# First block's output projection inside the sample scan, with the gate made chunk by chunk

## The chip, the core and the metric

The kernel runs on one core of a Trainium2 chip. A core has TensorE (PE, matrix products into PSUM), VectorE (DVE), ScalarE (ACT), GpSimd (POOL), and SyncE (SP), whose queue issues most of the DMAs here. The metric is the device time of one execution in microseconds. Where several executions were timed, the median is given.

## The reference

The reference is one layer of a diffusion backbone, for 256 prompt tokens and 1024 sample tokens of width 1024, with the same weights. The part that matters here is the mixer and the way it is added to the residual:

```python
proj = h @ w_in                                   # h = rmsnorm(x) * (1 + scale) + shift
hc, gb, gc, z, xbc, dtf, dtb = split(proj)
out_a = gb * dwconv1d(gc * hc, w_conv_short)      # 512 channels
xbc = silu(dwconv1d(xbc, w_conv_ssd, b_conv_ssd))
xs, bm, cm = split(xbc)
y_f, s_f = ssd_scan(xs, dt_f, a[0], bm, cm, init_f)
y_b, s_b = ssd_scan(reversed inputs, init_b)      # backward in position
y = y_f + reversed(y_b) + xs * d_skip
y = rmsnorm(y * silu(z), g_ssd_norm)              # "gate": over 512 channels
x = x + gate_m * (concatenate([out_a, y]) @ w_out)
h2 = rmsnorm(x, g_norm2) * (1 + scale_f) + shift_f
```

`ssd_scan` works in chunks of 128 positions: inside a chunk a decay-weighted product of C and B scores with x, from chunk to chunk a state that is decayed and added to. A feed-forward part with a depthwise convolution follows, and a final norm. Outputs are both token groups and two states.

## The kernel before

All operands lie with channels on partitions and tokens along the free axis. A projection splits each fp32 operand into a high and a low part in fp32r and makes three products (hi x hi, hi x lo, lo x hi). `mm3` issues them. `wload` loads a weight tile (`raw`, 128x1024), ACT copies its high half (`whi`), VectorE or GpSimd makes the low half (`wlo`).

The stages in order of time: norm of the inputs; the prompt's input projections; the sample's projections for x, B and C (`xbc`), with the conditioning products (`ada`) between them; the backward scan (`ssd_pass1`), which only stores chunk states; the forward scan (`ssd_pass2`), which makes the outputs; the gate; the output projection; the feed-forward part in two column groups.

`ssd_pass2` goes in half-chunk steps: a chunk of 128 tokens has two groups of four heads, and each is one step `i`, so the prompt has 4 steps and the sample 16. `front(c)` transposes a chunk's x and B, makes the scores and, with `state_step`, the next state. `prep(u, g)` loads `csb` (the cumulative log decays of eight rows, spread over all partitions by a DMA of 512 KB, two buffers), adds a mask into `wm`, takes exponentials on ACT and multiplies; `output(u, g)` makes 12 small matmuls into `yp` and VectorE adds them onto the tile `xs`. `prep` runs two steps ahead of `output`.

`fill(s, i)` is called ahead of each `output` and puts one more of the 16 remaining input projections (z and the three parts of the short convolution, made by the generator `fillers`) into the step, so that TensorE has work while the chain of `csb` runs. It does this at even `i` of the prompt and at `i % 3 != 2` of the sample. The rest of them follows the scan. The short convolution's result goes to DRAM as high and low parts (`oad`, tiles `xl`), the z projections as they are (`zd`).

After the scan `gate(s, behind)` works on whole token groups: it reads z back, applies Silu, multiplies, sums squares into one tile, takes the sum over channels by a matmul with ones, scales, and writes the high and low parts of y into SBUF tiles (`mya`, `myb`). Then `wout` makes the output projection in two column groups, A with 704 tokens and B with 576, eight output blocks each, from 16 operand tiles: eight of y, eight of the short convolution read back from `oad` (`oa`, `ob`). The residual x is loaded again (`x1`) to be added to. All these tiles come from pools that open when those of the scan close.

The order on each engine comes from a scheduler that works with priorities and with `after(mm, behind)`, which keeps a matmul behind another one. DMAs on a queue are issued in the order of its instructions, so a DMA that waits holds back those behind it.

The names that are used below: `wm`, `csb` (L562 to L573), `yp` (L592), `acc` (a projection's PSUM tile, L147 to L151), `gate` (L700 to L719), `oa`, `x1`, `ob` (L739, L742, L746).

Of the kernel before, what the change touches and what calls it, by code (L numbers as in the profile page):

```python
# [53 lines left out]
def body(nc, tc, A):  # L54
# [6 lines left out]
    def open_pool(name, side="left", **kw):  # L61
        g = tc.tile_pool(name=name, bufs=1, side=side, **kw)
        return g, g.__enter__()
# [53 lines left out]
    g_xy, xy = open_pool("xy", side="right")  # L117
# [24 lines left out]
    def mm3(outs, wh, wl, n):  # L142

        mms = []
        for k in range(n):
            for o, rh, rl in outs:
                nc.tensor.matmul(o, wh[:, k, :], rh(k), start=k == 0, stop=False)  # L147
            for o, rh, rl in outs:
                nc.tensor.matmul(o, wh[:, k, :], rl(k), start=False, stop=False)  # L149
            for o, rh, rl in outs:  # L150
                mm = nc.tensor.matmul(o, wl[:, k, :], rh(k), start=False, stop=k == n - 1)  # L151
            mms.append(mm)
        return mms
# [100 lines left out]
    def ada_block(k):  # L254
        wa = [T(xy, [P, 4, 2 * P], "xs", 4) for _ in range(2)]
        for i in range(2):
            dma(wa[i], A["w_ad1"][k, i])
        pm = psa()
        for j in range(KT):
            q = 32 * (j % 4)  # L260
            nc.tensor.matmul(pm[q:q + 32, 0:2 * P], sc[:, j, :], wa[j // 4][:, j % 4, :],
# [70 lines left out]
    oad = T(dr, [4, 2, P, TT], "oad", 1)  # L332
    zd = T(dr, [4, P, TT], "zd", 1)
# [38 lines left out]
    def zproj(s, j, lo_eng):  # L372
        pp = proj(s, 12 + j, lo_eng)
        z = T(cv, [P, s.T], "xl", 2)
        act(z, pp, AF.Copy)
        nc.scalar.dma_start(zd[j, :, s.t0:s.t0 + s.T], z)
# [105 lines left out]
    def tok_major(s, c, want_raw, r0):  # L482
# [10 lines left out]
        xd = T(sw[0], [P, 512], "xd", 4)  # L493
# [3 lines left out]
        if want_raw:  # L497
            xtok = T(sw[0], [P, 512], "xd", 4)
            act(xtok, xt, AF.Copy)
        return btok, xd, xtok  # L500

    def state_step(s, c, st, btok, xd, r0, tag):
        ad = psa()
        for g in range(2):
            nc.tensor.matmul(ad[:, g * 256:(g + 1) * 256], btok[:, g, :],
                             xd[:, g * 256:(g + 1) * 256], start=True, stop=True)
# [9 lines left out]
    def ssd_pass1(s):  # L516

        st = [None]

        def step(c):  # L520
            if st[0] is not None:
                dma(s.sbd[c], st[0])
            if c > 0 or s.name == "p":
                btok, xd, _ = tok_major(s, c, False, 32)
                st[0] = state_step(s, c, st[0], btok, xd, 32, "sb")
# [6 lines left out]
        return [lambda c=c: step(c) for c in range(s.nc - 1, -1, -1)]  # L532

    def ssd_pass2(s, fill):
# [7 lines left out]
        def front(c):  # L542
# [12 lines left out]
            if c < s.nc - 1 or s.name == "p":  # L555
                sf[0] = state_step(s, c, sf[0], btok, xd, 0, "sfw")
# [45 lines left out]
        for g in range(2):  # L602
            prep(u, g)
        for i in range(2 * s.nc):
            output(*us[i], fill(s, i))
# [19 lines left out]
    SS.X = [T(xy, [P, TS], "xs", 4) for _ in range(4)]  # L625
# [10 lines left out]
    silu = act(bcall, bcall, AF.Silu)  # L636
    for j in range(4):
# [8 lines left out]
    dts = dtstage(SS, d4_s, silu)  # L646
# [3 lines left out]
    SS.B, SS.C = bcs[0:2], bcs[2:4]  # L650
    for i in range(N_LOOP, 8):
# [3 lines left out]
        if i >= 4:  # L655
            ada(i - 2, lambda: T(nrm, [P, 1024], "x", 8))
# [3 lines left out]
    mask = sm[:, wff0:wff0 + 2 * L].rearrange("p (a l) -> p a l", a=2)  # L660
    dma(mask, A["cst"][:, 168:168 + 256].rearrange("p (a l) -> p a l", a=2))
    SP.mask = SS.mask = mask

# [9 lines left out]
    def fill(s, i):  # L673

        if i % 2 == 0 if s.name == "p" else i % 3 != 2:
            next(filler, None)
            return mid_mm[0]
        return last_mm[-1]

    for step in ssd_pass1(SS) + ssd_pass1(SP):  # L680
        step()
    ssd_pass2(SP, fill)
    ssd_pass2(SS, fill)
    for _ in filler:
# [3 lines left out]


    g_ya, ya = open_pool("ya")  # L690
    g_yb, yb = open_pool("yb")
    g_gt, gt_ = open_pool("gt")
    mya = [[T(ya, [P, TA], "ya", 8, F32R) for _ in range(2)] for _ in range(4)]
    myb = [[T(yb, [P, OB], "yb", 8, F32R) for _ in range(2)] for _ in range(4)]
    def gate(s, behind):
        n = s.T
        acc = T(gt_, [P, n], "gq", 3)
        for j in range(4):
            z = T(gt_, [P, n], "gz", 2)
            dma(z, zd[j, :, s.t0:s.t0 + n])  # L700
            act(z, z, AF.Silu)
            tt(s.X[j], s.X[j], z, ALU.mult)
            if j == 0:
                act(acc, s.X[j], AF.Square)
            else:
                q = T(gt_, [P, n], "gq", 3)
                sq = act(q, s.X[j], AF.Square)
                tt(acc, acc, q, ALU.add)
        r = T(gt_, [P, n], "gq", 3)
        rstd(r, acc, n, pst, 512, sq, behind)  # L710
        for j in range(4):
            y = s.X[j]
            stt(y, y, smv("gsd")[:, j:j + 1], r, ALU.mult, ALU.mult)
            parts = [(0, n, mya, s.t0)] if s.name == "p" else \
                [(0, TA - TP, mya, TP), (TA - TP, TS, myb, 0)]
            for a, b, dst, o in parts:
                hi = dst[j][0][:, o:o + b - a]
                act(hi, y[:, a:b], AF.Copy)  # L718
                tt(dst[j][1][:, o:o + b - a], y[:, a:b], hi.bitcast(F32), ALU.subtract)  # L719
    with tc.high_priority():  # L720
        gate(SP, last_mm[-5])
        gate(SS, last_mm[-3])
    close_pool(g_xy)

    close_pool(g_gt)
# [394 lines left out]
```

## Time and profile before

| | us |
|---|---|
| median of 3 runs | 1625.38 |
| lowest and highest | 1622.09, 1627.95 |
| the profiled execution, its own time | 1629.9 |
| its span in the profile | 1628.1 |
| granted TensorE clock, mean | 0.978 |

The profile is that of one execution of its own. The page gives busy time by engine; a window is a stretch of the span with the busy time of each engine in it; a row of waits tells which instruction waited, for which, how long in all, how often, and the longest. "PEclk" is the clock that TensorE was granted, as a share of the full one. "DMA share" is the mean busy share of the core's 16 DMA engines.

### The profile page before, as it was taken

Reading aid. Unit: us, or ns where it says so; the run is one execution under the profiler, and the core shown is the slowest. Engines: PE = TensorE matmul, PEld = TensorE weight load, DVE = VectorE, ACT = ScalarE, POOL = GpSimd, SP = SyncE. Lnnn points to the kernel's source line nnn. Section 1 sums busy time; section 2 is a strip of 40 time slices with the busy share of each in tenths; the row PEclk is TensorE's granted clock in tenths of the full one; section 3 lists DMA queues with packets and bytes.
Section 4 is the critical chain, followed back from the end, with each engine's and each line's share of the span. In section 5 each row is a group of like instructions: output and inputs, shape, how many; then the busy total and the mean of one; then the engine's idle time right before and its main releaser. Section 6 shows DMA issues by size and latency. Waiting matters only on the chain. (4 is left out here: it accounts for less than half of the span.)

```text
span 1628.1 us, 24939 instructions
## 1 busy us (share of the span) xinstructions
PE 1548.7 (95%) x9942; PEld 1411.9 (87%) x9942; DVE 1095.6 (67%) x1637; ACT 646.3 (40%) x1005; POOL 519.1 (32%) x288
## 2 busy tenths in 40 slices
PE   6989999888899799999999999999999999999997
PEld 2688767677777689999999999999999999999996
DVE  5664625445555636698666697656798777887685
ACT  6553534344445424343333353323334232433233
POOL 0445010011111000234434443434455444444442
PEclk8999999999999899999999999999999999999998
DMA  8555275534333551422222243222622223332221
GB/s 295 208 182 162 73 255 191 155 99 78 105 115 128 198 197 53 131 73 86 65 85 79 70 156 115 77 70 70 200 94 92 89 82 98 125 114 73 84 62 65
DMA packets 99534, 193.19 MB, mean 119 GB/s; under 512 B 9274, under 2 KB 51786, under 8 KB 99418
## 3 DMA queue, kind: packets, MB, share of 16 engines
q1 hardware_dynamic: 97690, 188.46, 35.9%
q10 hardware_dynamic: 1728, 3.15, 0.5%
q8 instruction: 78, 1.28, 0.3%
q14 instruction: 38, 0.31, 0.1%
HBM read 167.89 MB, written 23.67 MB: 118 GB/s over the span
## 5 line engine op out<-in xcount | busy, mean ns | idle before, releaser
L76 DVE SCALAR_TENSOR_TENSOR cc<-acc,sm,cc 128x384 f32<-128x384 f32 (+7 forms) x836 | 547.1, 665 | 114.8 <-ACT cc L855 44.9
L73 POOL TENSOR_TENSOR wlo<-raw,whi 128x1024 fp32r<-128x1024 f32 (+2 forms) x115 | 271.6, 2362 | 848.2 <-ACT whi L137 707.7
L137 ACT ACTIVATE whi<-raw 128x1024 fp32r<-128x1024 f32 x126 | 133.1, 1057 | 319.0 <-PE acc L149 279.6
L147 PE MATMUL acc<-ya,whi 128*128 128x256 f32 (+2 forms) x768 | 178.8, 315 | 10.7 <-ACT yb L718 7.7
L149 PE MATMUL acc<-ya,whi 128*128 128x256 f32 (+2 forms) x768 | 178.6, 314 | 0.0
L151 PE MATMUL acc<-ya,wlo 128*128 128x256 f32 (+2 forms) x768 | 177.7, 313 | 0.0
L149 PE MATMUL acc<-oa,whi 128*128 128x256 f32 (+2 forms) x768 | 176.3, 311 | 0.0
L151 PE MATMUL acc<-oa,wlo 128*128 128x256 f32 (+2 forms) x768 | 175.9, 311 | 0.0
L147 PE MATMUL acc<-oa,whi 128*128 128x256 f32 (+2 forms) x768 | 175.8, 311 | 0.0
L76 DVE SCALAR_TENSOR_TENSOR x<-dn,mod,x 128x320 f32<-128x320 f32 (+2 forms) x176 | 96.1, 546 | 91.8 <-PE dn L151 91.1
L147 PEld LDWEIGHTS acc<-ya,whi 128*128 128x128 f32 x768 | 138.8, 191 | 14.0 <-ACT yb L718 8.1
L149 PEld LDWEIGHTS acc<-ya,whi 128*128 128x128 f32 x768 | 139.5, 191 | 3.5 <-issue 0.2
L151 PEld LDWEIGHTS acc<-ya,wlo 128*128 128x128 f32 x768 | 139.1, 191 | 3.4 <-issue 0.2
L151 PEld LDWEIGHTS acc<-oa,wlo 128*128 128x128 f32 x768 | 137.6, 189 | 3.0
L147 PEld LDWEIGHTS acc<-oa,whi 128*128 128x128 f32 x768 | 137.5, 189 | 3.0
L149 PEld LDWEIGHTS acc<-oa,whi 128*128 128x128 f32 x768 | 137.5, 189 | 3.0
L73 POOL TENSOR_TENSOR dlo<-draw,dhi 128x512 fp32r<-128x512 f32 (+1 forms) x88 | 107.7, 1225 | 78.1 <-ACT dhi L912 78.1
L147 PE MATMUL acc<-h,whi 128*128 128x512 f32 x352 | 113.7, 404 | 3.8 <-DVE xs L76 3.8
L149 PE MATMUL acc<-h,whi 128*128 128x512 f32 x352 | 112.7, 399 | 0.0
L151 PE MATMUL acc<-h,wlo 128*128 128x512 f32 x352 | 112.4, 398 | 0.0
L147 PE MATMUL dn<-yb,dhi 128*128 128x320 f32 (+2 forms) x352 | 108.9, 309 | 1.8 <-DVE x L76 1.8
L151 PE MATMUL dn<-yb,dlo 128*128 128x320 f32 (+2 forms) x352 | 108.7, 309 | 0.0
(283 smaller groups left out, 3030.2 us busy)
## 6 DMA issues: line engine op xcount, KB each, us to landing
raw<-in_w_up SPq DMA_DIRECT2D x88, 512.0 KB, 3.5
x<-in_w_ada SPq DMA_DIRECT2D x32, 512.0 KB, 7.4
draw<-in_w_down SPq DMA_DIRECT2D x64, 256.0 KB, 2.8
x<-in_w_in SPq DMA_DIRECT2D x24, 512.0 KB, 4.0
raw<-in_w_in SPq DMA_DIRECT2D x22, 512.0 KB, 4.5
xs<-in_w_ad SPq DMA_DIRECT2D x16, 512.0 KB, 5.1
csb<-csds SPq DMA_DIRECT2D x16, 512.0 KB, 9.1
raw<-in_w_out SPq DMA_DIRECT2D x16, 512.0 KB, 3.6
```

What stands on the lines that cost most here:

```text
L73: (eng or V).tensor_tensor(out=out, in0=a, in1=b, op=op)
L76: V.scalar_tensor_tensor(out=out, in0=a, scalar=s, in1=b, op0=op0, op1=op1)
L137: act(hi, raw, AF.Copy)
L147: nc.tensor.matmul(o, wh[:, k, :], rh(k), start=k == 0, stop=False)
L149: nc.tensor.matmul(o, wh[:, k, :], rl(k), start=False, stop=False)
L151: mm = nc.tensor.matmul(o, wl[:, k, :], rh(k), start=False, stop=k == n - 1)
```

## The change

The gate of the sample is made per chunk inside the scan, its result goes to DRAM (`yd`, as high and low parts) and is read back as operand tiles. All 16 remaining projections stand in the backward scan and in the first half of the sample's forward scan. Group A of the output projection is cut into 32 quarter blocks of 12 matmuls, and three of them stand in each of the last eight sample steps. In detail:

- Pools get `reuse_waits="tile"`: a new tile waits for the old tiles in its place, not for all of a closed pool. `xy` moves to the left side, `xs` tiles come in pairs, the mask has a tile of its own, `xd` has 3 buffers and not 4, and the feed-forward part uses one pool `ma` of 16 tiles in the places of `ya` and `oa`.
- z gets its Silu right after its projection on ACT, and its store goes to SP's queue. The sample's dt stage stands behind the last of these Silu. The ada blocks stand at i = 2, 3, 5, 6 (before: 4 to 7).
- The backward scan runs the prompt first, in pairs of chunks with one projection between a pair's transposes and its state products. In the forward scan the state product comes behind the step's projection or output-projection step.
- `wlo` of group A is made on GpSimd; the order of the operand tiles is 4, 5, 6, 0, 1, 2, 3, 7.

```diff
     def open_pool(name, side="left", **kw):
+        if "space" not in kw:
+            kw["reuse_waits"] = "tile"
...
-        act(z, pp, AF.Copy)
-        nc.scalar.dma_start(zd[j, :, s.t0:s.t0 + s.T], z)
+        s.zact = act(z, pp, AF.Silu)
+        dma(zd[j, :, s.t0:s.t0 + s.T], z)
...
+        u.step(last_mm[-1])
         for i in range(2 * s.nc):
-            output(*us[i], fill(s, i))
+            behind = fill(i)
+            if i % 2 == 1 and i + 1 < 2 * s.nc:
+                u.step(behind)
+            output(*us[i], behind)
...
-    dts = dtstage(SS, d4_s, silu)
+    dts = dtstage(SS, d4_s, SP.zact)
...
+    ADA = {2: 2, 3: 3, 5: 4, 6: 5}
     for i in range(N_LOOP, 8):
...
-        if i >= 4:
-            ada(i - 2, lambda: T(nrm, [P, 1024], "x", 8))
+        if i in ADA:
+            ada_s(ADA[i])
...
+    def gate_chunk(c, hr):
+        cl = slice(c * L, (c + 1) * L)
+        tl = slice(TP + c * L, TP + (c + 1) * L)
+        zu = T(xy, [P, 8, L], "xp", 1, F32R)
+        z, u = zu[:, 0:4].bitcast(F32), zu[:, 4:8]
+        uf = u.bitcast(F32)
+        dma(z, zd[:, :, tl].rearrange("j p t -> p j t"))
+        for q in range(2):
+            tt(uf[:, 2 * q:2 * q + 2], xpair[q][:, :, cl], z[:, 2 * q:2 * q + 2], ALU.mult)
+        act(z, uf, AF.Square)
+        tt(z[:, 0:2], z[:, 0:2], z[:, 2:4], ALU.add)
+        pp = psa()
+        for i in range(2):
+            mm = nc.tensor.matmul(pp[:, 0:L], ones, z[:, i], start=i == 0, stop=i == 1)
+            if i == 0:
+                after(mm, last_mm[-1])
+        hi, r = hr[:, 0:4], hr[:, 4].bitcast(F32)
+        act(r, pp[:, 0:L], AF.Ln, scale=1.0 / 512, bias=epsc)
+        act(r, r, AF.Exp, scale=-0.5)
+        for j in range(4):
+            stt(uf[:, j], uf[:, j], smv("gsd")[:, j:j + 1], r, ALU.mult, ALU.mult)
+        act(hi, uf, AF.Copy)
+        tt(u, uf, hi.bitcast(F32), ALU.subtract)
+        for i, src in enumerate((hi, u)):
+            dma(yd[:, i, :, tl].rearrange("j p t -> p j t"), src.bitcast(F32))
+    KS_A = [4, 5, 6, 0, 1, 2, 3, 7]
+    def open_mix():
+        close_pool(g_cv)
+        close_pool(g_hs)
...
+        ph.mix = {k: mix_load(ph.ma, "ya", 16, TA, k, 0, TA) for k in KS_A}
+        ph.x1 = [T(ph.x1p, [P, TT], "x1", 8) for _ in range(KT)]
+        for k in range(KT):
+            dma(ph.x1[k], xT[:, k, :])
+    def wout_steps(mix, parts, t0, ks, alloc, eng, cuts):
+        x1 = ph.x1
+        for m in range(KT):
+            wh, wl = split_wout(m, eng)
+            pp = alloc()
+            for c in range(0, KT, cuts):
+                for k in ks[c:c + cuts]:
+                    st, sp = k == ks[0], k == ks[-1]
+                    for w, i, first, last in ((wh, 0, st, False), (wh, 1, False, False), (wl, 0, False, sp)):
+                        for p0, a, b, v in parts:
+                            mm = nc.tensor.matmul(pp[:, p0:p0 + b - a], w[:, k, :], mix[k][i][:, a:b],
+                                                  start=first, stop=last)
...
+                yield
+    N_PROJ = 8
+    N_FILL = 3
+    def fill_s(i):
+        if i == 0:
+            gate_p()
+        elif i % 2 == 0:
+            hr = T(cv, [P, 8, L], "cv", 4, F32R) if i <= N_PROJ else T(ph.gt, [P, 5, L], "hr", 1, F32R)
+            gate_chunk(i // 2 - 1, hr)
+        if i < N_PROJ:
+            project()
+            behind = mid_mm[0]
+        else:
+            if i == N_PROJ:
+                open_mix()
+                ph.steps = wout_steps(ph.mix, PARTS_A, 0, KS_A, pacc, PG, 2)
+            for _ in range(N_FILL):
+                next(ph.steps, None)
+            behind = last_mm[-1]
+        return behind
+    for i in range(0, len(scans), 2):
+        cps = [(step, c, copies(c)) for copies, step, c in scans[i:i + 2]]
+        project()
+        for (step, c, cp), behind in zip(cps, (mid_mm[0], last_mm[-1])):
+            step(c, cp, behind)
+    ssd_pass2(SP, lambda i: project() if i < 3 else last_mm[-1])
+    ssd_pass2(SS, fill_s)
+    gate_chunk(7, T(ph.gt, [P, 5, L], "hr", 1, F32R))
+    for _ in ph.steps:
+        pass
```

`mix_load` loads the high and low part of one operand tile, from `oad` for k from 4 on and from `yd` below; `gate_p` is the same gate on the prompt's 256 tokens.

How this moves instructions shows at three places. The first is SP's queue where the operand tiles and the residual are loaded. Before, they stand behind the gate, after the scan (`xl` is the last part of the short convolution, its store goes to `oad`):

```order
L746 DMA ob_4286<-oad_579 128x576
L398 DMA oad_579<-xl_4095 128x1024
L399 DMA oad_579<-xl_4097 128x1024
L739 DMA oa_4249<-oad_579 128x704
L739 DMA oa_4250<-oad_579 128x704
```

In the changed kernel the last rows of this load and the first rows behind it are, on the same queue, in the middle of the sample's scan (`ya` an operand tile, `x` the residual, `csb` the log decays of steps 10 and 11):

```order
L770 DMA ya_3952<-yd_572 128x704
L770 DMA ya_3954<-oad_571 128x704
L770 DMA ya_3956<-oad_571 128x704
L783 DMA x_624_3958<-in_xT 128x1280
L783 DMA x_625_3959<-in_xT 128x1280
L783 DMA x_626_3960<-in_xT 128x1280
L783 DMA x_627_3961<-in_xT 128x1280
L783 DMA x_628_3962<-in_xT 128x1280
L783 DMA x_629_3963<-in_xT 128x1280
L783 DMA x_630_3964<-in_xT 128x1280
L783 DMA x_631_3965<-in_xT 128x1280
L576 DMA csb_4051<-csds_569 128x8x128
```

So 16 operand tiles and eight residual tiles now stand ahead of the `csb` loads of the last six steps; before, no `csb` load stood behind either. The second place is TensorE ahead of the output of step 10. After the change the end of the output projection's fourth block (`acc_4363`) stands right ahead of that step's first matmuls:

```order
L796 MATMUL acc_4363<-ya_3956,whi_4359 128x256
L796 MATMUL acc_4363<-ya_3956,whi_4359 128x448
L796 MATMUL acc_4363<-ya_3954,wlo_4361 128x256
L796 MATMUL acc_4363<-ya_3954,wlo_4361 128x448
L606 MATMUL yp_4213<-wm_4053,xd_4046 64x128
L606 MATMUL yp_4213<-csb_4051,sfw_3862 64x128
```

Before, the first matmuls of group A stand behind the last input projection (`acc_4045`), which follows the scan and the gate's sums:

```order
L147 MATMUL acc_4045<-h_547,whi_4041 128x512 x2
L149 MATMUL acc_4045<-h_550,whi_4041 128x512 x2
L151 MATMUL acc_4045<-h_547,wlo_4043 128x512 x2
L147 MATMUL acc_4303<-ya_4112,whi_4299 128x256
L147 MATMUL acc_4303<-ya_4112,whi_4299 128x448
```

So half of group A now stands between the outputs of steps 9 and 10, and the other half around those of 10 to 15. The third place is TensorE from group A to group B (`ob`, `yb` operand tiles of B, `nacc` the squares of the second norm on A, `dn` their sum). Before, inside B's first block `acc_4863`:

```order
L151 MATMUL acc_4863<-yb_4126,wlo_4861 128x256
L151 MATMUL acc_4863<-yb_4126,wlo_4861 128x320
L147 MATMUL acc_4863<-ob_4281,whi_4859 128x256
L202 MATMUL dn_4778<-nacc_4753,ones_70 128x512
L202 MATMUL dn_4781<-nacc_4753,ones_70 128x192
L147 MATMUL acc_4863<-ob_4281,whi_4859 128x320
```

After (`sa_4664` is the sum of the last chunk's gate, from its squares `xp`):

```order
L796 MATMUL acc_4740<-ya_3954,wlo_4738 128x448
L744 MATMUL sa_4664<-xp_4658,ones_70 128x128 x2
L205 MATMUL dn_4865<-nacc_4840,ones_70 128x512
L205 MATMUL dn_4868<-nacc_4840,ones_70 128x192
L796 MATMUL acc_4950<-ob_4808,whi_4946 128x256
```

The norm's sum stood behind the first 25 matmuls of B; now both sums stand ahead of all of them. On SP's queue the loads of B's tiles stand behind the last chunk's stores to `yd`.

205 lines of the change are left out of this document (96 added, 109 removed).

## Prediction

> **What bounds the kernel now.** I read the page first, for the span and the share of TensorE.
>
> ```profile
> span 1628.1 us, 24939 instructions
> PE 1548.7 (95%) x9942; PEld 1411.9 (87%) x9942; DVE 1095.6 (67%) x1637; ACT 646.3 (40%) x1005; POOL 519.1 (32%) x288
> ...
> PEclk8999999999999899999999999999999999999998
> ```
>
> TensorE is busy for 95% of the span, nearly always at full clock. So the only time to win is where it waits or runs at half clock, and the next view has to say where that is: the busy time of each engine by stage. I cut at the start of the backward scan (258), of the sample's second scan (320), at its end (511), at the wait ahead of the output projection (547), at the projection's two column groups A (555.2) and B (624.9), and at the feed-forward part (676.8).
>
> ```profile
> core 0: us, PE busy (x) PEld busy (x) DVE busy (x) ACT busy (x) POOL busy (x), PEclk, DMA share, GB/s
> ...
> 160.00:258.00 98.00, 94.25 (x474) 65.96 (x472) 41.29 (x58) 39.23 (x43) 7.16 (x3) 0.97 0.52 183
> 258.00:320.00 62.00, 57.52 (x334) 45.56 (x332) 40.34 (x63) 28.80 (x67) 4.73 (x2) 1.00 0.49 153
> 320.00:511.00 191.00, 167.99 (x977) 135.23 (x976) 102.06 (x129) 80.64 (x175) 30.80 (x11) 0.96 0.35 95
> 511.00:547.00 36.00, 34.65 (x147) 27.17 (x146) 22.72 (x30) 24.71 (x34) 0.00 (x0) 1.00 0.44 147
> 547.00:555.20 8.20, 0.48 (x3) 0.09 (x2) 8.20 (x11) 5.29 (x10) 0.00 (x0) 0.67 0.68 216
> 555.20:624.90 69.70, 66.71 (x384) 63.15 (x385) 23.94 (x31) 13.72 (x16) 0.00 (x0) 0.92 0.54 201
> 624.90:676.80 51.90, 51.90 (x389) 51.34 (x388) 41.03 (x61) 26.48 (x36) 4.79 (x2) 1.00 0.25 80
> 676.80:1628.00 951.20, 938.42 (x6359) 917.69 (x6357) 721.62 (x1126) 342.55 (x507) 408.93 (x237) 0.99 0.30 93
> ```
>
> From 258 to 624.9 TensorE stands idle for 4.48 + 23.01 + 1.35 + 7.72 + 2.99 = 39.6 us. The granted clock adds to that: 0.96 in the scan costs 0.04 x 191 = 7.6 us, 0.92 in group A 0.08 x 69.7 = 5.6 us. Together **52.8 us** lie there, and group B has none. The feed-forward part keeps its order on every engine, so it moves as a block. TensorE's waits of 258 to 690 name the causes:
>
> ```profile
> PE yp L592 <- DVE wm L73: 9.0, 4, 5.8
> PE acc L147 <- ACT yb L718: 7.7, 1, 7.7
> PE yp L592 <- DVE xs L76: 7.2, 5, 2.2
> PE yp L592 <- DVE csb L73: 3.1, 5, 0.6
> PE acc L147 <- ACT whi L137: 3.0, 1, 3.0
> ```
>
> Columns are the waiter, the releaser, total us, times, the longest. The scan's outputs (yp) wait for the decay weights (wm, csb); the output projection waits once for the gate's last split (7.7) and once for a weight tile that lands behind the x loads (3.0).
>
> **The change, part by part.** *What goes.* Gating chunk by chunk takes the 7.7 us wait away; projections and output-projection steps in all 16 sample steps cover the yp waits. I take out the whole 52.8 us and then add what is left or new.
>
> *Ahead of the scan.* Three waits stand here now:
>
> ```profile
> PE acc L147 <- DVE xs L76: 3.8, 1, 3.8
> PE sa L475 <- DVE cv L472: 3.4, 1, 3.4
> PE acc L147 <- ACT xl L375: 3.3, 1, 3.3
> ```
>
> ```profile
> L370 ACT ACT_TABLE_LOAD x3 | 3.8, 1283 | 8.4 <-DVE xs L76 8.1 <-DVE bc L76 0.4
> ```
>
> Silu on the z projections, between the Ln and Exp of the sample's dt stage, makes six more table loads on ACT: at worst 6 x 1.283 = 7.7 us, if TensorE waits for all of them. At best the 3.4 and the 3.3 shrink, since the dt stage stands behind the last Silu and its reader later. Four ada blocks begin two steps earlier, and the weights of one stand on SP's queue behind a store that waits for VectorE. I take **+2**, with -4 and +8 as ends: ACT is busy 39.23 of 98 us in that stage, so most loads find room.
>
> *Gate sums.*
>
> ```profile
> L202 PE MATMUL yp<-gq,ones x6: 379/592/697, 520.8 to 543.0; 128*128 128x512 f32 x4, 128*128 128x256 f32 x2
> ```
>
> These sum the squares now; the new gate adds only pairs on VectorE and lets TensorE do the other half, on twice the columns. Some 4 x 0.56 us come to **+2.2**.
>
> *Backward scan and first half.* Each of the first eight sample steps now has a projection, and the state products stand behind it.
>
> ```profile
> L147 PE MATMUL acc<-h,whi 128*128 128x512 f32 x166 | 52.9, 400 | 0.0
> ```
>
> ```profile
> 369.01:379.89 10.88, 10.88 (x48) 8.93 (x48) 6.38 (x6) 2.22 (x4) 2.87 (x1) 1.00 0.49 122
> ```
>
> One projection is 48 matmuls and 10.88 us. The scan window holds 3 x 166 of them, 10.4 projections; 167.99 less the 7.6 of slow clock is 160.4, and without 10.4 x 10.88 there remain 47.2 us for 16 steps: 2.95 us of own work a step. With a projection that makes 13.8 us, in which one csb load and its exponentials fit. The idle time here is 27.5 us now, mostly in steps without a projection; I leave **+4** of it (0 to 15, if the queue also makes these steps late).
>
> *Second half.* Group A is 66.71 - 5.6 = 61.1 us, 7.64 for each of its eight output blocks and 1.91 a quarter. Eight steps of 2.95 + 3 x 1.91 and eight quarters after them are 84.7 us of work. What stands against it is SP's queue. Ahead of the csb loads of steps 10 to 15 there are 16 mix tiles and eight x tiles:
>
> ```profile
> x<-in_xT SPq DMA_DIRECT2D x8, 640.0 KB, 10.7
> oa<-oad SPq DMA_DIRECT2D x8, 352.0 KB, 4.4
> oad<-xl SPq DMA_DIRECT2D x2, 512.0 KB, 3.0
> ```
>
> ```profile
> 562.70:582.90 20.20, 20.20 (x129) 19.32 (x128) 5.44 (x9) 3.44 (x4) 0.00 (x0) 1.00 1.02 406
> ```
>
> Such loads move 406 GB/s with every DMA engine busy. 16 x 352 + 8 x 640 KB are 11.0 MB, 27 us. Seven weight tiles, two stores of the long convolution, eight of gated chunks and a few state and z tiles are about 8.1 MB, 20 us. A csb load (512 KB in pieces of 128 numbers) is another matter:
>
> ```profile
> 423.33 0.37 SPq L562 DMA_DIRECT2D csb<-csds  x1
> ...
> 427.93 0.37 SPq L562 DMA_DIRECT2D csb<-csds  x1
> ```
>
> ```profile
> 432.10 1.23 DVE L73 TENSOR_TENSOR wm<-csb,sm 128x1024 f32<-128x1024 f32 x1 [3.83 <-DMA csb<-csds]
> ...
> 435.91 0.69 DVE L73 TENSOR_TENSOR wm<-wm 128x512 f32<-128x512 f32 x1 [1.72 <-ACT wm L570]
> 438.10 1.23 DVE L73 TENSOR_TENSOR wm<-csb,sm 128x1024 f32<-128x1024 f32 x1 [1.50 <-DMA csb<-csds]
> ```
>
> ```profile
> DMA to landing us min/median/max: 5.7/8.9/10.4
> ```
>
> ```profile
> 458.00:460.00 2.00, 0.26 (x3) 0.29 (x4) 2.00 (x4) 0.88 (x1) 2.00 (x1) 1.00 0.38 82
> ```
>
> Two that were issued 4.6 us apart landed 6.0 us apart (their readers waited for them), and a lone one takes 8.9. So a csb holds the queue for 6.0 to 8.9 us. Seven of them from the eighth projection on, with 27 + 20 us of other traffic, land by 89 to 109 us. From a landing to the weights takes some 5.2 us (432.10 to 435.91 + 0.69 and one like it), then half a step, 1.5, and the 55 matmuls of A behind the last output, 8.8. A so ends at 104.5 to 124.8 against 84.7 of work: a stall of 20 to 40. I take **+24**, near the pair's 6.0, with some 4 us for loads that wait for a buffer.
>
> The Trainium skill ("DMA: Bandwidth & Descriptors", Specifications) puts the smallest transfer for line rate at 512 bytes, which is just what a csb piece has. By it a csb would go at 406 GB/s, 512 KB in 1.3 us, seven in 9, and the time would be near that of the first rival below. The trace has 82 GB/s while one runs alone, and disagrees.
>
> *From A to B.* The order of TensorE now has the last gate's sum and the norm's sum ahead of the first matmul of B, and SP has B's 16 tiles behind the last chunk's stores.
>
> ```profile
> DMA to landing us min/median/max: 3.7/4.4/8.0
> ```
>
> This is the read-back of the oa tiles. The gate of 128 columns, its split and the stores stand ahead: bounded by nothing and by the 7.7 us that the gate of 1024 columns costs now. With at least 3.7 behind it and the norm's sum, 8 to 13, and I take **+10**.
>
> *Clock.*
>
> ```profile
> 327.90:334.70 6.80, 5.52 (x35) 5.22 (x36) 4.95 (x8) 4.87 (x10) 2.83 (x1) 0.50 0.23 80
> 590.70:597.50 6.80, 6.18 (x21) 5.79 (x22) 3.13 (x4) 2.57 (x3) 0.00 (x0) 0.50 0.49 154
> ```
>
> After a wait of 5.8 and one of 3.0 us the granted clock was 0.50 for 6.8 us, which costs up to 3.4 us. Where the queue sets the pace a slow TensorE loses nothing. The one after A counts: **+4** (0 to 7).
>
> *At nothing.*
>
> ```profile
> L73 POOL TENSOR_TENSOR wlo<-raw,whi 128x1024 fp32r<-128x1024 f32 (+2 forms) x115 | 271.6, 2362 | 848.2 <-ACT whi L137 707.7
> ```
>
> Low halves of A's weights go to POOL: 2.36 us under 7.64 of matmuls; were that cover gone, 8 x 2.36 would show. The z stores on SP's queue, the pools' finer waits and the earlier load of wff lie under projections.
>
> **Sum:** -52.8 + 2 + 2.2 + 4 + 24 + 10 + 4 = **-6.6 us** on the profiled execution's 1629.9, that is 1623.3. This execution is 0.28% over the median of the runs (1625.38), so I scale: **1618.8**.
>
> **The rivals.** *Transfers overlap.* With a csb at a DMA share of 0.38, wide loads could travel beside it. Four of A's blocks stand ahead of the output of step 10 on TensorE, 30.6 us in which its csb may come. What stalls then is the mix: 27 us of loads, before which two blocks and the outputs of steps 8 and 9 have some 18 us to do: 10 instead of 24. That is -20.6: 1609.3, scaled 1604.8. Against it: in the pair above the second csb was late.
>
> *Each wait cools the clock.* Two of the second half's waits are followed by a window at 0.50 that nothing covers: 2 x 3.4 more, +0.2 in all: 1630.1, scaled 1625.6. For it speak the two rows above, against it that the queue then sets the pace. The Trainium skill ("TensorE: Matmul & The Clock Gate", What's actually happening) has the clock halved after an idle window of some 3.4 us until as long a busy one; by it a wait costs 1.7 us and not 3.4, and the result would lie between this and mine. The trace's windows are twice that long.
>
> *The csb loads set the pace (slower).* There are two csb buffers, so a load is issued only when a step's outputs have been made. If the full 8.9 us stand in each of seven steps, the stall is 40: +9.4, 1639.3, scaled 1634.8. The point from which it turns is a price where 24 + 6.6 us are lost: 6.0 + (30.6 - 20)/7 = 7.5 us a csb, inside the bounds. Then the wait for the gate has only moved to the csb. In the same way the change may not do what it says: four blocks in one piece ahead of step 10 are not three quarters a step, and that is in the price already.
>
> **How the numbers follow.** Forecast 0.35, overlap 0.24, clock 0.15, csb 0.26. The forecast is 0.4% below the median; a measurement of this kernel can tell 0.3%, 4.9 us. Some 0.12 of the forecast's own chance falls within that and 0.02 above; of the clock's, 0.11 within, 0.02 each side; of csb's, 0.03 within. Faster 0.47, within 0.26, slower 0.27. The range takes the overlap with low ends elsewhere (some 11 us less, 1594) and the csb case with a late first half (some 9 more, 1644).
>
> **What would show it.** After: no wait of output-projection matmuls for the gate's split in A; sample steps 0 to 7 of some 14 us each with little idle time; waits of the A matmuls for mix tiles, then of yp for wm at step 10, some 24 us in all; a csb landing over 20 us after its issue behind the x loads; 8 to 13 us with almost no matmul between A and B; B near 52 us. Wrong would be: idle time in the second half under 12 or over 35 us, or over 8 in the first, or a feed-forward part that is not 951 us long.

## The result and the profile after

| | before | after |
|---|---|---|
| median, us | 1623.74 (4 runs, 1621.57 to 1627.95) | 1673.15 (4 runs, 1670.45 to 1674.81) |
| ratio of the two | | 1.030 (95% interval 1.027 to 1.033) |
| span in the profile, us | 1628.1 | 1673.0 |

The change makes the kernel 3% slower: +49 us on the medians, +44.9 on the two profiled spans. The forecast was -6.6 and the range ended at 1644. The page of the changed kernel:

```profile
span 1673.0 us, 25070 instructions
PE 1556.9 (93%) x9972; PEld 1415.8 (85%) x9972; DVE 1102.1 (66%) x1666; ACT 651.5 (39%) x1014; POOL 537.0 (32%) x296
```

TensorE's share fell from 95 to 93%, and its busy time rose by 8 us although nearly the same matmuls run: a sign of a slower clock, to which I come back. The windows of the changed kernel, cut at the same events as before: the start of the backward scan (261.2), the end of the eighth projection of the sample's scan (524.0), the end of group A (659.8), the start of B (672.2) and its end.

```profile
261.20:524.00 262.80, 233.84 (x1202) 189.67 (x1201) 124.25 (x162) 93.89 (x179) 39.18 (x16) 0.95 0.37 111
524.00:659.80 135.80, 103.16 (x659) 89.00 (x657) 72.39 (x112) 49.35 (x106) 16.91 (x6) 0.86 0.55 169
659.80:672.20 12.40, 3.56 (x10) 1.71 (x9) 8.94 (x17) 8.92 (x14) 0.00 (x0) 0.68 0.43 134
672.20:728.10 55.90, 54.56 (x384) 53.81 (x385) 35.95 (x53) 19.42 (x26) 4.80 (x2) 0.92 0.42 142
728.10:1673.00 944.90, 932.51 (x6358) 911.65 (x6356) 720.75 (x1126) 342.25 (x507) 408.79 (x237) 1.00 0.30 94
```

The columns are those of the windows of before. From the scan's start to the end of A it takes 398.6 us, before 366.9 (258 to 624.9); the start is 3.2 later; from A to B there are 12.4 us that were not there; B takes 4.0 longer; what follows B to the end of the span takes 944.9, before 951.3, 6.4 less. 3.2 + 31.7 + 12.4 + 4.0 - 6.4 = 44.9. TensorE's waits, first from 261 to 524, then from 524 on:

```profile
PE sa L744 <- DVE xp L75: 20.1, 3, 9.0
PE sa L715 <- DVE cv L75: 5.4, 1, 5.4
```

```profile
PE yp L606 <- DVE wm L75: 17.5, 3, 8.4
PE sa L744 <- DVE xp L75: 9.1, 3, 3.4
PE acc L796 <- DMA ya<-oad: 6.6, 1, 6.6
PE acc L796 <- DMA ob<-oad: 5.1, 1, 5.1
```

In the first half the outputs no longer wait. The sums of the gate wait in their place: L715 is the prompt's, L744 that of a chunk. One of them in detail, on TensorE, VectorE and SP's queue:

```profile
464.52 1.22 PE L744 MATMUL sa<-xp,ones 128*128 128x128 f32 x4 [8.95 <-DVE xp L75]
```

```profile
457.56 0.42 DVE L75 TENSOR_TENSOR xp<-xs,xp 128x256 f32<-128x256 f32 x1
462.90 1.23 DVE L75 TENSOR_TENSOR wm<-csb,mask 128x1024 f32<-128x1024 f32 x1 [4.92 <-DMA csb<-csds]
464.04 0.42 DVE L75 TENSOR_TENSOR xp<-xp 128x256 f32<-128x256 f32 x1
```

```profile
454.09 0.35 SPq L137 DMA_DIRECT2D raw<-in_w_out  x1
454.53 0.39 SPq L576 DMA_DIRECT2D csb<-csds  x1
```

Read upwards: the csb load is issued at 454.53 and lands by 462.9. The mask add that needs it stands on VectorE ahead of the gate's last add (464.04), so that add waits too, and with it the sum on TensorE, which stands in the middle of a projection. The remaining 22 matmuls of that projection could have run and are held up. In the kernel before, VectorE waited for csb as well (258 to 547; total, times, longest), but no input projection waited in the scan; TensorE's rows of waits, which stand in the prediction, name the outputs and group A:

```profile
DVE wm L73 <- DMA csb<-csds: 56.7, 15, 7.2
```

In the changed kernel these waits sum to 68.7 us in 14 from 261 to 660, 41.5 of them in the first half.

### The profile page after: what moved, and what is told of

It reads as the page before. It is cut to its first block, busy times and chain, and to the rows that moved or that the text cites. A ratio compares the mean times of both kernels' runs of the same rounds, so it can differ in the third digit from the quotient of the medians.

```text
span 1673.0 us, 25070 instructions
## 1 busy us (share of the span) xinstructions
PE 1556.9 (93%) x9972; PEld 1415.8 (85%) x9972; DVE 1102.1 (66%) x1666; ACT 651.5 (39%) x1014; POOL 537.0 (32%) x296
## 5 line engine op out<-in xcount | busy, mean ns | idle before, releaser
L75 POOL TENSOR_TENSOR wlo<-raw,whi 128x1024 fp32r<-128x1024 f32 (+2 forms) x123 | 289.2, 2352 | 868.7 <-ACT whi L139 665.2
L152 PE MATMUL acc<-ya,whi 128*128 128x256 f32 (+2 forms) x1408 | 319.9, 308 | 0.0
L150 PE MATMUL acc<-ya,whi 128*128 128x256 f32 (+2 forms) x1408 | 319.2, 307 | 0.0
L154 PE MATMUL acc<-ya,wlo 128*128 128x256 f32 (+2 forms) x1408 | 319.2, 307 | 0.0
L152 PEld LDWEIGHTS acc<-ya,whi 128*128 128x128 f32 x1408 | 249.7, 188 | 5.3 <-issue 0.2
L154 PEld LDWEIGHTS acc<-ya,wlo 128*128 128x128 f32 x1408 | 249.6, 188 | 5.4 <-issue 0.2
L150 PEld LDWEIGHTS acc<-ya,whi 128*128 128x128 f32 x1408 | 249.2, 188 | 4.6
L150 PE MATMUL dn<-yb,dhi 128*128 128x320 f32 (+2 forms) x352 | 108.9, 309 | 1.9 <-DVE x L78 1.9
L152 PE MATMUL dn<-yb,dhi 128*128 128x320 f32 (+2 forms) x352 | 108.6, 308 | 0.0
L994 ACT ACTIVATE dhi<-draw 128x512 fp32r<-128x512 f32 (+1 forms) x88 | 53.0, 602 | 117.3 <-PE dn L152 52.9
L152 PE MATMUL dn<-g,dhi 128*128 128x320 f32 (+2 forms) x304 | 93.8, 309 | 0.5 <-POOL g L75 0.5
L150 PE MATMUL dn<-g,dhi 128*128 128x320 f32 (+2 forms) x304 | 93.8, 309 | 0.0
L154 PE MATMUL dn<-g,dlo 128*128 128x320 f32 (+2 forms) x304 | 93.7, 308 | 0.0
L150 PEld LDWEIGHTS acc<-h,whi 128*128 128x128 f32 x352 | 66.5, 193 | 18.5 <-issue 3.6
```

Of the source, the lines that this page charges most:

```text
L75: (eng or V).tensor_tensor(out=out, in0=a, in1=b, op=op)
L150: nc.tensor.matmul(o, wh[:, k, :], rh(k), start=k == ks[0], stop=False)
L994: act(wh, raw, AF.Copy)
```

## The experiments

All start from the changed kernel unless said otherwise. Each was timed beside the kernel before, so the ratios to that are what is compared; the changed kernel's is 1.030 (1.027 to 1.033), and 0.003 are 5 us.

### The gate's front on GpSimd

```diff
-            tt(uf[:, 2 * q:2 * q + 2], xpair[q][:, :, cl], z[:, 2 * q:2 * q + 2], ALU.mult)
+            tt(uf[:, 2 * q:2 * q + 2], xpair[q][:, :, cl], z[:, 2 * q:2 * q + 2], ALU.mult, PG)
         act(z, uf, AF.Square)
-        tt(z[:, 0:2], z[:, 0:2], z[:, 2:4], ALU.add)
+        tt(z[:, 0:2], z[:, 0:2], z[:, 2:4], ALU.add, PG)
```

> The changed kernel with one edit: the two products with z and the sum of squares' add ahead of each chunk's gate sum run on GpSimd, not on VectorE. Theory (the gate sum on TensorE stands inside a projection and waits for that add, which stands on VectorE behind a mask add that waits for a csb load): the three waits of 4 to 9 us for the sum in the first half (21 us in the changed kernel's profile, and slow clock behind them) go, so the time falls by 20 to 32 us, to 1641 to 1653. Rival (the csb loads set the pace of a step anyway): the same time is then waited by the scan's outputs for wm, and the time changes by less than 6 us.

Measured: 1678.77 us, ratio 1.033 (1.030 to 1.035): no gain. The sums wait as long, now for GpSimd (first row, TensorE from 80 to 760), and GpSimd itself waits (second row):

```profile
PE sa L744 <- POOL xp L75: 29.9, 7, 10.7
```

```profile
458.81 0.72 POOL L75 TENSOR_TENSOR xp<-xs,xp 128x256 f32<-128x256 f32 x1 [3.54 <-DVE xs L78]
```

The product needs the chunk's last outputs (`xs`), which VectorE had finished late for the same reason: until 446.66, 12 us earlier, it had stood 9.60 us for a csb load. So the place of one add is not the cause; in the chunk that is shown, VectorE's work ahead of it is late too.

### The gate sum one step later

```diff
         elif i % 2 == 0:
-            hr = T(cv, [P, 8, L], "cv", 4, F32R) if i <= N_PROJ else T(ph.gt, [P, 5, L], "hr", 1, F32R)
-            gate_chunk(i // 2 - 1, hr)
+            ph.rest = gate_chunk(i // 2 - 1)
+            if i == N_PROJ:
+                ph.rest(T(cv, [P, 8, L], "cv", 4, F32R))
...
+        if i % 2 == 1 and i > 1 and i != N_PROJ + 1:
+            ph.rest(T(cv, [P, 8, L], "cv", 4, F32R) if i < N_PROJ else T(ph.gt, [P, 5, L], "hr", 1, F32R))
```

`gate_chunk` now ends behind the add of the squares and returns the rest: sum, scaling, split and stores.

> The changed kernel with one edit: each chunk's gate sum and what follows from it are issued one half-chunk step later (chunk 3 excepted, which must be stored before the operand tiles are read), so that the sum stands behind the next projection; VectorE still makes the add. Theory (an order problem: TensorE meets the sum too early): the waits for the sum go here too, time down by 20 to 32 us, as in the run with GpSimd. Rival (csb loads set the pace): within 6 us of the changed kernel. If GpSimd helps and this does not, VectorE's queue and not the place on TensorE is what counts.

Measured: 1669.29 us (1660.64 to 1672.39), ratio 1.026 (1.023 to 1.030), some 4 to 6 us less, which the two intervals do not tell from nothing: the rival's size. The profile caught the fastest of these runs, with a span 14.1 us shorter. In it the scan starts at 259.8 and the eighth projection ends at 507.7, so the first half takes 247.9 us, 14.9 less. Then group A meets an operand tile that has not landed:

```profile
528.69 0.96 PE L799 MATMUL acc<-ya,whi 128*128 128x256 f32 x2 [14.99 <-DMA ya<-oad]
```

Even so the second half is no longer than in the changed kernel (131.6 us to 135.8); from A to B it takes 18.7 us where it took 12.4. So the first half gave 15 of the 20 us or more that the theory asked for, and the profiled run kept nearly all of that. The other three runs are 8 to 12 us slower than this one, and no trace shows where.

### The residual's loads spread over steps 9 to 15

```diff
-        for k in range(KT):
-            dma(ph.x1[k], xT[:, k, :])
...
+            for k in {9: [0, 1], 10: [2], 11: [3], 12: [4], 13: [5], 14: [6], 15: [7]}.get(i, []):
+                dma(ph.x1[k], xT[:, k, :])
```

> The changed kernel with one edit: the eight loads of the residual x are not issued in one piece at sample step 8 but two at step 9 and one at each of steps 10 to 15. Theory (operand tiles and x loads ahead of the csb loads of steps 10 and 11 on SP's queue make TensorE wait 8 us for wm at step 10): the csb of step 10 lands 10 to 13 us earlier, its wait falls under 3 us, time down by 8 to 14 us. Rival (csb's own price of 6 to 9 us each sets the pace of the second half): the wait moves to steps 12 to 15, less than 4 us in all.

Measured: 1671.29 us, ratio 1.028 (1.026 to 1.030): no difference that can be told. The waits of yp for wm did fall, from 17.5 to 3.6, but TensorE then waits for the residual that comes later (`acc<-ya` behind the PSUM tile that VectorE empties with x):

```profile
PE acc L794 <- DVE x L78: 6.6, 1, 6.6
PE acc L794 <- DMA ya<-oad: 6.4, 1, 6.4
PE yp L606 <- DVE wm L75: 3.6, 1, 3.6
```

The wait that the prediction foresaw is there (csb behind x); its removal is worth nothing that these runs can tell.

### The dt stage where it was

```diff
-    dts = dtstage(SS, d4_s, SP.zact)
+    dts = dtstage(SS, d4_s, silu)
```

> The changed kernel with one edit undone: the sample's dt stage stands behind the Silu of B and C again, not behind the last Silu of the z projections. Theory of the prediction (the part ahead of the scan costs some 2 to 3 us, by this order and its table loads): 1 to 4 us faster. Rival (it was moved off a path that waits): 2 to 8 us slower.

Measured: 1676.96 us, ratio 1.032 (1.030 to 1.035): no faster, so the theory falls. It is some 4 us slower, but the intervals overlap: the rival is neither shown nor excluded.

### Three csb buffers

```diff
-        new = T(sw[0], [P, 512], tag, 3 if tag == "sb" else 3)
+        new = T(sw[0], [P, 512], tag, 3 if tag == "sb" else 2)
...
-            sf[0] = T(sw[0], [P, 512], "sfw", 3)
+            sf[0] = T(sw[0], [P, 512], "sfw", 2)
...
-            csb = T(sw[0], [P, 8, L], "csb", 2)
+            csb = T(sw[0], [P, 8, L], "csb", 3)
...
-    dma(sm[:, wff0:wff1], A["sm"][:, wff0:wff1])
-    mask = T(sw[0], [P, 2, L], "mask", 1)
+    mask = sm[:, wff0:wff0 + 2 * L].rearrange("p (a l) -> p a l", a=2)
...
+    dma(sm[:, wff0:wff1], A["sm"][:, wff0:wff1])
```

> The changed kernel with three csb buffers, not two; to make room the forward state has two tiles and not three, and the mask lies in the place of wff again, which is loaded after group B. What the last runs left: with the gate's front on GpSimd the sum waited as long, since VectorE's and SP's work of the chunk came late as well. Theory (a loop through the csb load: it is issued only when an output has freed its buffer, VectorE waits 9 to 10 us for it in order, and the chunk's outputs, gate products and the next csb issue all stand behind): one more buffer lets the load go a step earlier, VectorE's waits for csb in the first half fall from 9 to 10 us to under 4, and the time falls by 15 to 35 us. Rival (the buffer is not what delays the issue; SP's queue is, by stores and weight loads that wait ahead of it): less than 5 us.

Measured: 1637.76 us, ratio 1.008 (1.006 to 1.010): 35 us less. VectorE's waits for csb up to the end of the eighth projection, first with two, then with three buffers:

```profile
DVE wm L75 <- DMA csb<-csds: 41.5, 8, 10.3
```

```profile
DVE wm L75 <- DMA csb<-csds: 13.1, 2, 10.5
```

The two that are left stand at 379 and 388 us, ahead of the first chunk's gate; behind it none is left in the first half. The gate's sums stand where they stood, and TensorE's waits for them in the first half fall from 20.1 and 5.4 us to:

```profile
PE sa L743 <- DVE xp L75: 4.4, 2, 4.1
PE sa L714 <- DVE cv L75: 1.4, 1, 1.4
```

Windows with three buffers, cut at the same events as the changed kernel's:

```profile
261.00:503.70 242.70, 229.45 (x1202) 186.90 (x1201) 126.80 (x164) 96.28 (x181) 38.05 (x16) 0.98 0.43 120
503.70:624.80 121.10, 96.81 (x659) 86.19 (x657) 69.24 (x110) 47.03 (x102) 15.83 (x6) 0.90 0.64 185
624.80:637.20 12.40, 3.58 (x9) 1.70 (x8) 8.28 (x16) 8.44 (x13) 0.00 (x0) 0.72 0.50 151
637.20:691.40 54.20, 53.79 (x384) 53.23 (x385) 36.59 (x54) 20.19 (x28) 4.80 (x2) 0.94 0.42 146
691.40:1637.40 946.00, 933.64 (x6358) 913.03 (x6357) 720.54 (x1126) 342.21 (x507) 408.75 (x237) 1.00 0.30 94
```

The first half is 20.1 us shorter and has 13.3 us of idle time where it had 29.0; the second is 14.7 shorter, with 24.3 where it had 32.6.

The control, the same room-making edits with two csb buffers:

> The control to three csb buffers: the changed kernel with the edits that made room for the third (two forward states, mask in the place of wff) but still two csb buffers. Theory (the buffer brought the 35 us): within 5 us of the changed kernel's 1673. Rival (the mask's place or the later wff load brought part of it): 8 us faster or more.

Measured: 1679.38 us, ratio 1.032 (1.030 to 1.035): no faster. The 35 us are the buffer's.

### The stores of y on ACT's queue

```diff
-            dma(yd[:, i, :, tl].rearrange("j p t -> p j t"), src.bitcast(F32))
+            nc.scalar.dma_start(yd[:, i, :, tl].rearrange("j p t -> p j t"), src.bitcast(F32))
```

> The changed kernel with one edit: the stores of each gated chunk go to ACT's DMA queue, not to SP's. Theory (these stores wait on SP's queue for the gate's split, and the csb loads and z loads behind them are issued late by that): csb loads of the first half are issued 2 to 5 us earlier, and the time falls by 5 to 15 us. Rival (csb buffers or VectorE's order set the pace): less than 4 us either way.

Measured: 1673.35 us, ratio 1.031 (1.029 to 1.033): nothing. These stores on SP's queue are not what the time hangs on.

### No gate in the scan

```diff
     def fill_s(i):
-        if i == 0:
-            gate_p()
-        elif i % 2 == 0:
...
+    gate_p()
+    for c in range(8):
+        gate_chunk(c, T(cv, [P, 8, L], "cv", 4, F32R))
+    open_mix()
+    ph.steps = wout_steps(ph.mix, PARTS_A, 0, KS_A, pacc, PG, 2)
```

> The changed kernel with the gate and the output projection taken out of the scan: all chunks are gated after it, then group A runs; the eight projections stay in the first eight sample steps. Looked at is the first half, from the first gate sum's place at 387 us in the changed kernel to the end of the eighth projection at 524, 137 us with 27 us of waits for gate sums. Theory (the gate's sums couple the projections to the csb chain): the first half has under 8 us of waits in all and is 30 us shorter or more. Rival (csb loads set a step's pace even beside a projection): waits of yp for wm of over 15 us take their place. Of the whole time nothing is claimed, since the second half then has nothing to fill its steps: the csb chain alone should give steps of 9 us or more.

Measured: 1744.01 us in all. The eighth projection ends at 505.8, 18 us sooner (30 were expected). TensorE's waits from 372 to 506:

```profile
PE sa L562 <- DVE wm L75: 15.2, 5, 6.2
```

The gate's sums are gone, and the first half is 18 us shorter. That is the price of the whole gate there, its products, loads and stores with it, and not of the sums alone. In their place the scores of a chunk wait for a PSUM tile that VectorE has not read yet, since it waits for csb (once 11.95 us, with TensorE's wait of 6.2 behind it). Theory and rival each had a part.

### Three csb buffers in the kernel before

```diff
-        xd = T(sw[0], [P, 512], "xd", 4)
+        xd = T(sw[0], [P, 512], "xd", 3)
...
-            sf[0] = T(sw[0], [P, 512], "sfw", 3)
+            sf[0] = T(sw[0], [P, 512], "sfw", 2)
...
-            csb = T(sw[0], [P, 8, L], "csb", 2)
+            csb = T(sw[0], [P, 8, L], "csb", 3)
```

> The kernel before with three csb buffers (xd with three and the forward state with two tiles to make room). Theory (there, VectorE's 51 us of waits for csb held back little that TensorE needed soon, so the buffer is worth less than in the changed kernel): 4 to 16 us faster, at most the 19 us that the outputs wait for wm, xs and csb now. Rival (the csb loop is as dear there): 25 us faster or more; second rival (no use at all, its waits are of the order on VectorE): within 3 us.

Measured: **1598.57 us** (1597.69 to 1599.95), 0.984 of the kernel before (0.983 to 0.986): 26 us faster, and the fastest of all the kernels here. The rival holds: the loop through csb was nearly as dear before. VectorE's waits for csb in the scan are 16.8 us here, where they were 56.7. No control with the smaller `xd` and state alone was run for this kernel. The windows of this kernel: the scan from its start (256.3) to the end of the last projection, the wait for the gate, group A, group B, and what follows B:

```profile
256.30:517.90 261.60, 251.25 (x1455) 202.08 (x1453) 170.47 (x220) 135.64 (x275) 31.09 (x13) 1.00 0.49 126
517.90:526.00 8.10, 0.39 (x3) 0.07 (x1) 8.10 (x11) 5.19 (x10) 0.00 (x0) 0.79 0.68 220
526.00:594.40 68.40, 65.38 (x384) 61.52 (x385) 23.93 (x31) 13.68 (x16) 0.00 (x0) 0.95 0.56 205
594.40:646.40 52.00, 52.00 (x390) 51.47 (x389) 41.02 (x61) 26.52 (x36) 4.79 (x2) 1.00 0.26 81
646.40:1597.10 950.70, 937.68 (x6359) 917.23 (x6357) 721.49 (x1126) 342.22 (x507) 408.48 (x237) 1.00 0.29 93
```

The scan in the kernel before:

```profile
258.00:547.00 289.00, 260.15 (x1454) 207.96 (x1453) 165.13 (x220) 134.15 (x275) 35.53 (x13) 0.97 0.39 114
```

The same work takes 27.4 us less, of which 18.5 are idle time (28.9 to 10.4) and 8.9 are busy time, with the granted clock at 1.00 where it was 0.97. The waits cost more than they last, since the clock is lower around them.

### Three buffers and the later sum; and B's tiles early

> Three csb buffers and the gate sum one step later, together. With three buffers there are 16.5 us of waits for the sum left. Theory (with csb out of the way, what is left is that TensorE meets the sum before VectorE can have it): 6 to 14 us faster than with three buffers alone, 1624 to 1632. Rival (the waits only move, as with two buffers, where the later sum brought 4 us): 0 to 4 us.

Measured: 1633.31 us, ratio 1.006 (1.004 to 1.007), some 4 us less than with three buffers alone, with overlapping intervals: the rival. On top of it, the tiles of B that come from the short convolution are loaded ahead of the last gate:

```diff
+    close_pool(g_sw)
+    close_pool(g_sd)
+    g_ob, ob = open_pool("ob", side="right")
+    mixb = {k: mix_load(ob, "ob", 8, TB, k, TA, TB) for k in KS_B if k >= 4}
     gate_chunk(7)(T(ph.gt, [P, 5, L], "hr", 1, F32R))
...
```

> The kernel of the run before it (three csb buffers, gate sum late), and the eight operand tiles of group B that come from the short convolution are loaded ahead of the last chunk's gate, into the place of the closed scan pools. Theory (the 12 us from A to B are the wait for these loads behind the last chunk's stores): that gap falls under 4 us, the time by 7 to 12 us against the run before it. Rival (the gap is the norm's sum and the last gate, not the loads): under 3 us.

Measured: 1637.22 us, ratio 1.008 (1.006 to 1.010), 4 more. The gap from A to B does fall, from 10.1 to 2.4 us, but B itself takes 64.6 us where it took 53.3, and stops in its middle for 3.7 and 3.5 us. The time did not go, it moved.

### Group A half a chunk later, and without a quota

```diff
-    N_PROJ = 8
+    N_PROJ = 9
...
-    ssd_pass2(SP, lambda i: project() if i < 3 else last_mm[-1])
+    ssd_pass2(SP, lambda i: project() if i < 2 else last_mm[-1])
```

> The kernel with three csb buffers, and one projection moved from the prompt's scan into step 8 of the sample's: the output projection then starts at step 9, half a chunk later behind the gate of chunk 3. Theory (with three buffers the largest waits left, 4.4 and 8.6 us for operand tiles, and the slow clock of 0.90 behind them, come from starting group A right behind the gate of chunk 3, whose stores and the tile loads behind them it must wait for): those waits fall under 5 us together and the time by 6 to 14 us against three buffers alone (1637.8). Rival (the tile loads take their 27 us whenever they start, and the wait only moves by a step): less than 4 us.

Measured: 1632.94 us, ratio 1.006 (1.004 to 1.008), 4 to 5 less than with three buffers alone, with overlapping intervals: close to the rival. The tile waits did fall to one of 5.3 us, but the outputs wait for wm again; TensorE from 258 to 740:

```profile
PE yp L606 <- DVE wm L75: 20.0, 3, 10.7
PE acc L795 <- DMA ya<-oad: 5.3, 1, 5.3
```

With three csb buffers and `N_FILL = 0`:

> The kernel with three csb buffers, and group A without a quota in the scan: its steps are issued behind the last chunk's gate and only the scheduler pulls them forward (its order on TensorE still has four of the eight blocks ahead of the sums of chunk 4 and later). Theory (what the quota of three quarters a step does is small beside the loads): within 6 us of three buffers alone (1637.8). Rival (the quota is what fills the steps): 10 us slower or more.

Measured: 1632.91 us, ratio 1.005 (1.003 to 1.007), 5 less: the theory. The quota of three quarters a step brings nothing that shows; the scheduler pulls A forward without it.

## Why the prediction was wrong

The sum again, each term as predicted and as the windows show it. Idle time is a window less TensorE's busy time in it. The clock's term follows from busy time: 395.1 us from the scan's start to B's end now, 379.2 before, 15.9 more; less the sums' 2.2, with before's 13.2, that is 26.9.

| term | forecast | measured |
|---|---|---|
| idle and slow clock of before, taken out | -52.8 | -52.8 |
| ahead of the scan | +2 | +3.2 |
| gate sums (taken over) | +2.2 | +2.2 |
| idle, scan's start to the eighth projection | +4 | +29.0 |
| idle, second half | +24 | +32.6 |
| idle, A to B and in B | +10 | +10.2 |
| slow clock | +4 | +26.9 |
| behind B | 0 | -6.4 |
| sum | -6.6 | +44.9 |

**What bounds the kernel** was read rightly, and the terms ahead of the scan and from A to B hold. Two of the prediction's own signs of being wrong came: over 8 us of idle time in the first half (29.0), and a feed-forward part that is not 951 us long (944.9).

**The first step that failed** is "I leave +4 of it (0 to 15 ...)" for the first half. I counted a step's own work and a projection, 13.8 us, and found that a csb load fits. It does, but the gate's sum put a wait for VectorE into the middle of the projection: 25.5 of the 29.0 us are waits of the gate's sums (20.1 and 5.4). I had priced the sum by its columns alone (+2.2) and not asked what stands ahead of its input on VectorE: a mask add that waits for csb. Taking the gate out shortens the first half by 18 us, and moving the sum a step back by 15. With a third csb buffer the sums stay where they are, and their waits there fall from 25.5 to 5.8 us. So the csb loads, by way of VectorE, are what made the sums wait.

**The second** is "Where the queue sets the pace a slow TensorE loses nothing." The granted clock was 0.50 in five stretches of the second half:

```profile
534.50:548.15 13.65, 6.55 (x23) 5.32 (x22) 5.21 (x10) 5.38 (x14) 0.00 (x0) 0.50 0.72 188
585.70:592.53 6.83, 3.11 (x23) 2.74 (x24) 6.79 (x11) 5.80 (x12) 1.44 (x1) 0.50 0.13 53
595.94:602.77 6.83, 5.70 (x20) 4.53 (x20) 3.60 (x9) 2.20 (x5) 0.79 (x1) 0.50 0.56 158
619.83:626.66 6.83, 5.54 (x20) 4.38 (x21) 5.91 (x5) 2.30 (x6) 2.78 (x1) 0.50 0.21 63
647.14:650.55 3.41, 3.41 (x24) 3.15 (x24) 1.36 (x2) 1.92 (x4) 0.00 (x0) 0.50 0.02 6
```

TensorE is busy for 24.3 us in them, and half of that, 12.2 us, is lost. Five more such stretches, four in the first half and one around the wait from A to B, hold 27.6 us of busy time. Together 25.9 us are lost, close to the 26.9 of the table. That this comes on top of the idle time and does not hide in it, three csb buffers show: the second half's idle time falls by 8.3 us and its busy time by 6.4 with it. So does the kernel before with three buffers: 18.5 us of waits gone took 8.9 us of busy time with them. This was my second rival's mechanism, priced at two windows of 3.4 us. The Trainium skill ("TensorE: Matmul & The Clock Gate", What's actually happening) has the clock halved after an idle window of some 3.4 us. The trace agrees in the main: four of the five stretches begin in a wait of 3.4 us or more or right behind it, the first one behind a wait of 2.37.

**The second half's idle time** was mis-sized, 32.6 for 24. The waits that the prediction named do make 24.1 us: 6.6 for an operand tile, 17.5 of yp for wm. The rest is for the most part gate sums again, 5.8 us. That the 24 was hit so well is partly luck: no single wait carries it, and the wait at step 10 is one of three for wm. It came as foreseen: the two csb loads behind the x loads were issued from 560.31 on, and the output waited 8.4 us for wm.

```profile
560.31 7.27 SPq L576 DMA_DIRECT2D csb<-csds  x2
```

```profile
577.23 1.23 DVE L75 TENSOR_TENSOR wm<-csb,mask 128x1024 f32<-128x1024 f32 x1 [3.09 <-DMA csb<-csds]
```

```profile
589.04 0.66 PE L606 MATMUL yp<-wm,xd 128*64 128x128 f32 x2 [8.37 <-DVE wm L75]
```

But spreading the x loads gained nothing, so this queue was one late thing among several.

**The slower rival** had the right part, the two csb buffers, and the wrong place: I looked for it in the second half, while its loop costs in the whole scan. A third buffer is worth 35 us in the changed kernel and 26 in the one before. So it explains little of the difference between the two: with three buffers each, they stand at 1637.76 and 1598.57, still 39 us apart.

**What stays open** is the cause of these 39 us. The windows say where they lie, 40.3 us between the two profiled spans: 4.7 ahead of the scan, 25.7 from its start to the end of A (363.8 against 338.1), 12.4 from A to B, 2.2 in B, and 4.7 less behind it. In the 25.7 there are 16.5 us of idle time. With three buffers the kernel before has left, as its largest waits there, the gate's (7.7) and the weight tile's (3.0), so the change has little left to win, while the changed kernel still has 13.3 us idle in its first half, 24.3 in its second at a clock of 0.90, and a stretch of 12.4 us from A to B. Of the edits tried on it (later sum, later start, no quota, earlier loads for B) each brought 5 us at most, and where the rows were read another wait had come up. That the second half is short of cover as a whole, with 5.7 us of matmuls a step where the first has 10.9, and operand tiles to load besides, fits all of this but was not shown by a run of its own.

## What to carry to other kernels

When work is moved under a loop for cover, ask of each instruction that it puts on the covering engine what stands ahead of its input on the engine that makes it; a covering stream with one wait in it covers nothing behind that wait. An engine that waits in order for a load holds back all that stands behind it, and one more buffer for that load can be worth more than a new arrangement: here 26 us in the kernel before, with one more buffer for csb and one fewer each for `xd` and the forward state. When an edit removes a wait, look for it in the next row before counting the gain: four edits here removed the wait that they aimed at (sum late, x spread, B's tiles early, A later), and the median time moved by 6 us or less.

## What was not expected of the hardware

The part behind B has the same instructions in the same order on TensorE, yet takes 944.9 to 946.0 us in the changed kernel and its three-buffer version, and 950.7 to 951.3 in the kernel before and its own. TensorE's idle time there is nearly the same (12.4 and 12.9 us); its busy time is 5.9 us less. The gain is spread, not in one place: 200 us without a gap hold 1461 matmuls before (1176.8 to 1376.8) and 1474 after (1228.1 to 1428.1). Operands lie at other places in SBUF, in one pool of 16 tiles and not two of eight; whether that is the cause was not tried.

A csb load in the second half took 16.9 us from issue to landing (560.31 to the mask add at 577.23), behind eight x loads that had been issued ahead of it. The median of all csb loads was 8.9 before and 9.6 after. (The prediction calls the 8.9 that of a lone load; it is the median of all 20.)
